# Forgetting attention's raw weights in ten large buffers, and the weights' bound by GpSimd's queue

## The chip, the cores and the metric

The kernel runs on one core of a Trainium2 chip. Its time is that of the device, in microseconds (us): the median of several runs of the whole program. Five engines work side by side, each through its own queue in order: TensorE (PE, matrix products), VectorE (DVE), ScalarE (ACT), GpSimd (POOL) and SyncE (SP, which here only issues transfers). An instruction waits at the head of its queue for the semaphores it names; what stands behind it waits too.

## The reference: what is computed

Two layers over a sequence of 1024 tokens with 1024 channels, batch 1. Each layer projects `x` into a main part, queries for the memory and gates, computes a main branch and a memory branch, multiplies both by the gates, projects back and normalises:

```python
h = x @ w_in                      # [u_main | q_mem | g_main | g_mem], 3072 columns
y_main = main_fn(u_main)
y_mem = memory_attention(q_mem, mem, w_mem_kv)       # 4 heads, 256 memory tokens
y = concat([y_main * silu(g_main), y_mem * silu(g_mem)])
x = layer_norm(ALPHA * x + y @ w_out)
```

In layer 0 `main_fn` is a pooling over the last 2, 4, 8 and 16 tokens by groups of 256 channels, with a linear map for each group. Then `x @ w_kv_shared` gives keys, values and the logits of the forget gates for 16 heads of 64 channels. In layer 1 `main_fn` is forgetting attention: `logit[t, s] = q_t . k_s / 8 + cum[t] - cum[s]`, causal, where `cum` is the running sum of the logarithms of the forget gates.

## The kernel before

**Products in parts.** A float32 product is made as a sum of products of parts: a value is cut into a high part and a rest. In layer 0 that is `hi` with `lo` and `top` (`hi_lo`: a cast on ACT, a subtraction on DVE L187, a cast on ACT L188). In layer 1 both operands are scaled by powers of two and cut into two 16-bit halves (`Half`); the scale of the weights, `sw`, comes from a bound on all of that layer's weights.

**A slab** (L272) is 128 columns of a projection for all 1024 tokens: the weights come as two pieces of 128x512 float32, 256 KB each, and 48 products of 512 columns (L294) go to two banks of PE's accumulators (`pj`), 24 to each. `split_w` (L195) loads a piece by SP's queue into `raw`, a ring of four buffers of 2 KB a partition (L114), and cuts it into `w`, a ring of six (L117).

**The bound** (`look_ahead` L219, `bound_of` L231). The 84 pieces of weights behind the bound are loaded once more ahead of their use: each comes into `raw` by SP (L223), and ACT takes absolute values with their sum (L224, an instruction and a read of its accumulator). They are called for in portions: five behind each slab of memory queries (L412), three at each step of the memory attention, three behind a gate's slab, six behind a group, and what is left at the bound itself. `bound_of` then reduces them on DVE, writes a column to DRAM (L236), reads it back to all partitions (L238) and reduces again. `scales_of` (L244) calls it at the start of layer 0's output projection (L558), ahead of its products (L534).

**Layer 0** does pooling group 0, the memory attention, pooling groups 1 to 3 and the output projection; the weights of the projection are cut ahead of time in portions of 4, 12 and 12 (`out_proj.split`) into buffers that are free (`wtags`). **Layer 1** does the memory attention, then the forgetting attention (`fox`, 16 heads in 8 pairs). There a flag `low[0]` makes POOL cut the weights (`gp_scaled_hi_lo`): it scales a piece in place (L170), copies the high half (L181) and subtracts (L172). 27 slabs are cut so: keys, values and queries of the pairs, and their gates. POOL also makes the causal masks in `R` (L884), which the custom instruction on DVE that adds the decay to the logits waits for (L892); ACT takes the exponential (L900), ACT and DVE make two 16-bit halves (L921, L922), SP issues their transposes `T<-P` (L935), and PE multiplies by the values (L944).

**Order.** Forgetting attention and memory attention run under a schedule in which PE's order is written by hand: the products of the slabs are spread between the heads' steps (`Fill.pump`), and the gates of pairs 3, 5 and 6 (`late_gate`) fill the last pair's steps. The orders of the other engines come from a scheduler that works on the program as a whole. Ten buffers named `B` of 4 KB a partition serve layer 1: results of the memory attention's queries, and at the end the weights of the output projection.

Of the kernel before, what the change touches and what calls it, by code (L numbers as in the profile page):

```python
# [18 lines left out]
P = 128  # L19
# [54 lines left out]
def trunk_kernel(ctx, tc, x, xT, memT, win, wk, wv0, wv, wmk, wmv, wout, poolw, pscale, lng, lnb, bforget, out):  # L74
# [39 lines left out]
    def raw(shape):  # L114
        return sb(list(shape), "raw", 4)
# [7 lines left out]
    def w_slots(tags, where):  # L123

        def tiles(k):
            tag, bufs = tags[k]
            if tag == "w":
                return [parts_of(wt, [P, NH]) for _ in range(2)]
            two, four = [P, 2, NH], [P, 2, 2, NH]
            if tag == "MK":  # L130
# [61 lines left out]
        nc.gpsimd.tensor_tensor(to.lo, src, to.hi.bitcast(F32), ALU.subtract)  # L192
        gp_copy(to.top, src)

    def split_w(src_dram, shape, sc=None):  # L195
        r = raw(shape)
        nc.sync.dma_start(r, src_dram)
        if sc is not None:
            to = half_of(wt, shape)
            (gp_scaled_hi_lo if low[0] else scaled_hi_lo)(to, r, sc)  # L200
            return to
        to = parts_of(wt, shape)
        (gp_hi_lo if low[0] else hi_lo)(to, r)
        return to
# [11 lines left out]
    sums = const.tile([P, len(ahead)], F32, name="sums")  # L216
    seen_of = iter(enumerate(ahead))

    def look_ahead(n):  # L219

        for k, src in islice(seen_of, n):
            r = raw(list(src.shape))
            nc.sync.dma_start(r, src)  # L223
            nc.scalar.activation(r, r, AF.Abs, accum_out=sums[:, k : k + 1])  # L224

    def power_of(to, m, least):

# [2 lines left out]

    def bound_of(m):  # L231

        look_ahead(len(ahead))
# [10 lines left out]
    def scales_of(gb):  # L244

        other = tiny(1)
        nc.vector.tensor_reduce(tmp, gb[0], AX.X, ALU.max, apply_absolute_value=True)
        nc.vector.tensor_reduce(other, gb[1], AX.X, ALU.max, apply_absolute_value=True)
        nc.vector.tensor_tensor(tmp, tmp, other, ALU.add)
        nc.vector.tensor_scalar(tmp, tmp, 32.0, None, ALU.mult)  # L250
        power_of(ex, tmp, 2.0 ** -2)
        nc.vector.reciprocal(sx, ex)
        nc.vector.tensor_scalar(sx, sx, 2.0 ** 13, None, ALU.mult)
        m = tiny(1)
        bound_of(m)
# [16 lines left out]
    def slab(pieces_dram, X, evac, banks=("pj", 2)):  # L272

        arrived = isinstance(pieces_dram, list)
        sc = sw if isinstance(X, Half) else None
        ws = list(pieces_dram) if arrived else [split_w(pieces_dram[0], [P, 4, P], sc)]
        accs = {}
        high, low_top = (0,), (1, 2)
        if arrived:
            order = [(n, pc, part) for pc in range(2) for n, part in ((0, high), (1, high), (1, low_top), (0, low_top))]  # L280
        else:
            order = [(0, pc, part) for part in (high, low_top) for pc in range(2)]
            order += [(1, pc, part) for part in (low_top, high) for pc in range(2)]
        seen = {0: 0, 1: 0}
        for n, pc, part in order:
            if len(ws) <= pc:
                ws.append(split_w(pieces_dram[pc], [P, 4, P], sc))
            if n not in accs:
                accs[n] = ps([P, NH], *banks)
            for i in part:  # L290
                a, b = three(ws[pc], X)[i]
                for k in range(4):
                    seen[n] += 1
                    nc.tensor.matmul(  # L294
                        accs[n], a[:, k, :], b[:, pc * 4 + k, n * NH : (n + 1) * NH],
                        start=seen[n] == 1, stop=seen[n] == 3 * KT,
                    )
                    if seen[n] == 3 * KT:
                        evac(slice(n * NH, (n + 1) * NH), accs[n])
                    yield NH  # L300
# [99 lines left out]
    def mem_attention(l, X, kv, qtile, ytile, yd):  # L400
# [6 lines left out]
        for h in range(MH):  # L407
            while turns:
                spread()
            q = parts_of(qtile, [P, S])  # L410
            run(slab(win[l, 8 + h], X, lambda cols, acc: q_split(l, q[:, cols], acc)))
            look_ahead(5)  # L412
            qs.append(q)
            if not l:
                keys(h)
            vals(h)
# [45 lines left out]
        with tc.manual_schedule(engines={PE}):  # L462
            for t in range(ST + 2):
                todo = [MVALUES if k in (5, 9) else 0 for k in range(t, ST + 2)]
                part = max(0, (fill.left + sum(todo)) / len(todo) - todo[0])
                if t < ST:
                    probs(t)
                look_ahead(3)
                fill.pump(part * 0.4)
                for h in range(MH):  # L470
                    if todo[0]:
                        values((t - 5) // 4, h)
                    fill.pump(part * 0.15)
            fill.pump(float("inf"))
# [4 lines left out]
    class OutProj:  # L479
# [3 lines left out]

        def __init__(self, l, wtile, yd):
            self.l, self.wtile, self.yd, self.ws, self.accs = l, wtile, yd, [{}, {}], None
            self.raws, self.n = [], 0

        def fetch_two(self, land):

# [29 lines left out]
        def products(self, accs, c, ys, apart=False):  # L519

            high, low_top = (0,), (1, 2)
            if apart:
                order = [(a, nh, part) for a in range(2) for part in (high, low_top) for nh in range(2)]
            else:
                order = [
                    (a, nh, part) for part in ((low_top, high) if c == 0 else (high, low_top))
                    for a in range(2) for nh in range(2)
                ]
            for a, nh, part in order:
                for i in part:  # L530
                    for k in range(4):
                        kt = 4 * c + k
                        y, w = three(ys[:, k, a * P : (a + 1) * P], self.ws[nh][kt // 2][kt % 2])[i]
                        nc.tensor.matmul(  # L534
                            accs[a][nh], y, w, start=kt == 8 and i == 0, stop=kt == 7 and i == 2,
                        )
                        yield NH

        def early(self, y, ys):
# [10 lines left out]
        def rest(self, resid, X, dst):  # L550
# [13 lines left out]
            for sp, c in order + [(sp, c) for sp in range(2, ST // 2) for c in (2, 0, 1)]:  # L564
# [5 lines left out]
                for k, _ in enumerate(self.products(accs[sp], c, ys, X is None and sp == ST // 2 - 1 and c == 1)):  # L570
                    if c != 2 and k % 6 == 5:
                        spread()
                if c == 1:
                    norm(sp, accs.pop(sp), gb, resid, X, dst)

# [56 lines left out]
    y1d = dram.tile([3, P, 4, S], F32, name="y1d")  # L632

    with tc.tile_pool(name="in0", bufs=1) as in0:

        def bt(shape=(P, S), dt=F32R):
            return sb(list(shape), "B", 8, dt, in0)

        def pool_group(g):
# [25 lines left out]
            for f in (2 * g, 2 * g + 1):  # L665
                y = sb([P, S], "Y", 4, F32, in0)
                run(gate_units(win[0, 12 + f], y, X))
                if g:
                    look_ahead(3)
                ys.append(y)  # L670
            for d in range(2):
                f = 2 * g + d
# [19 lines left out]

        X1 = half_of(stream, [P, KT, S])
        out_proj.rest(x, X1, x1)
# [3 lines left out]
    with tc.tile_pool(name="in1", bufs=1) as in1:  # L698
# [432 lines left out]
```

## Time and profile before

| what | value |
|---|---|
| median of 3 runs | 1254.48 us (1251.09 to 1254.51) |
| the profiled execution | 1255.45 us |
| its span | 1253.7 us |
| granted clock of PE, mean over the span | 0.986 |
| PE / DVE / ACT / POOL busy | 95% / 65% / 58% / 17% |
| the 54 scales of POOL (L170) | 38.9 us busy, 123.6 us idle ahead of them |

The profile is one execution. Busy shares are means over stages with different limits: layer 0 takes the first 490 us or so (the last transposes of its result, L376, start at 492.8; the output projection begins at 344), forgetting attention lies between about 640 and 1130 us. In a row of a group stand the line, the engine, the operation, the result and its source, the shape, the count, the busy time, the mean duration in ns, and the idle time of the engine just ahead with what ended it. In a row of waits stand the waiting engine, its line and the releaser, then the total in us, the count and the longest. In a timeline's row stand the start, the duration, the engine, the operation and the count, and in brackets the idle time ahead of it. SPq is SP's queue, where a transfer is issued.

### The profile page before, as it was taken

What the parts mean: (1) busy time and instruction counts of PE and PEld (TensorE: products, weight loads), DVE (VectorE), ACT (ScalarE), POOL (GpSimd) and SP (SyncE); (2) the same over time, 40 slices, a digit from 0 to 9 for tenths busy, and PEclk for the clock granted to TensorE, in tenths of its full rate; (3) what the DMA queues carried; (4) which work ended last, traced back from release to release, by engine and by line L of the source; (5) the groups of instructions that cost most, each with busy time, mean ns of one, the idle gap of its engine ahead of it and who ended that gap; (6) DMA issues with size and microseconds to landing.
All of it is one profiled execution on the core that took longest, in us unless ns stands there. A gap on an engine that the chain in (4) does not pass through costs nothing. (4 is left out here: it accounts for less than half of the span.)

```text
span 1253.7 us, 20190 instructions
## 1 busy us (share of the span) xinstructions
PE 1185.7 (95%) x6970; PEld 685.0 (55%) x7018; DVE 811.0 (65%) x1882; ACT 730.3 (58%) x1596; POOL 218.9 (17%) x349
## 2 busy tenths in 40 slices
PE   8999998999999998999998989999998988999997
PEld 4566665555555556556664445544444454455553
DVE  7544656564735557357655887868877798773753
ACT  6577985675733235457323776767665776685220
POOL 4000000000000000000023443443443434440000
PEclk9999999999999999999999999998999999999999
DMA  6356885545573323345515787967886897886331
GB/s 227 108 181 190 211 211 176 182 138 186 163 202 101 105 108 129 96 134 103 166 55 144 155 161 176 184 144 160 158 173 136 177 181 172 200 225 203 134 139 46
DMA packets 279799, 195.61 MB, mean 156 GB/s; under 512 B 213776, under 2 KB 228368, under 8 KB 279696
## 3 DMA queue, kind: packets, MB, share of 16 engines
q1 hardware_dynamic: 279696, 194.31, 59.5%
q8 instruction: 55, 0.90, 0.3%
q14 instruction: 48, 0.39, 0.1%
HBM read 116.08 MB, written 22.61 MB: 111 GB/s over the span
## 5 line engine op out<-in xcount | busy, mean ns | idle before, releaser
L294 PE MATMUL pj<-A,w 128*128 128x512 f16 (+2 forms) x2908 | 674.1, 385 | 8.3 <-DVE A L822 2.9
L294 PEld LDWEIGHTS <-w 128*128 128x128 f16 (+1 forms) x2592 | 249.7, 98 | 291.8 <-issue 14.7
L900 ACT ACTIVATE T<-MK,s 128x512 f32<-128x512 f32 x192 | 111.0, 578 | 49.3 <-DVE P L922 27.2
L921 ACT ACTIVATE P<-T,s 128x512 f16<-128x512 f32 x192 | 102.6, 576 | 55.6 <-issue 19.5
L922 DVE SCALAR_TENSOR_TENSOR P<-T,s,P 128x512 f16<-128x512 f32 x192 | 111.4, 612 | 27.2 <-ACT P L921 25.0
L534 PEld LDWEIGHTS <-T 128*128 128x128 bf16 x736 | 71.0, 98 | 86.5 <-issue 6.3
L187 DVE TENSOR_TENSOR w<-raw,w 128x512 bf16<-128x512 f32 x84 | 59.8, 713 | 69.7 <-ACT w L186 48.8
L795 POOL MEMSET G<- 128x128 f32 x1 | 0.2, 205 | 597.8 <-PE T L270 597.8
L270 PE MATMUL L<-A 128*128 128x512 f16 (+3 forms) x384 | 86.0, 327 | 14.1 <-DVE s L892 13.9
L892 DVE CUSTOM_DVE_ANT_0 MK<-L,R,scales 128x512 f32<-128x512 f32 (+3 forms) x128 | 80.3, 627 | 9.5 <-PE L L270 5.9
L224 ACT ACTIVATE raw<-raw 128x512 f32<-128x512 f32 (+1 forms) x84 | 51.2, 610 | 57.5 <-DMA raw<-in_wv_dram 20.1
L294 PEld LDWEIGHTS pj<-A,w 128*128 128x128 f32 x368 | 69.0, 190 | 20.1 <-ACT A L186 3.1
L944 PE MATMUL O<-T,V 128*64 128x128 f16 (+1 forms) x1152 | 59.1, 224 | 15.3 <-DMA T<-P 13.1
L270 PEld LDWEIGHTS <-A 128*128 128x128 f16 x384 | 37.2, 98 | 58.6 <-issue 18.7
L944 PEld LDWEIGHTS <-V 128*64 128x64 f16 (+1 forms) x1152 | 52.2, 106 | 29.4 <-DMA T<-P 13.3
L186 ACT CAST T<-T 128x1024 fp32r<-128x1024 f32 x23 | 24.1, 1047 | 70.0 <-DMA T<-y1d 34.8
L172 POOL TENSOR_TENSOR w<-raw,w 128x512 f16<-128x512 f32 x54 | 63.3, 1173 | 3.7
L884 POOL TENSOR_SCALAR_AFFINE_SELECT R<-R 128x128 f32<-128x128 f32 x128 | 39.9, 317 | 131.1 <-DVE s L892 88.9
L187 DVE TENSOR_TENSOR T<-T,T 128x1024 bf16<-128x1024 f32 x23 | 28.0, 1218 | 50.9 <-ACT T L186 33.5
L186 ACT CAST w<-raw 128x512 fp32r<-128x512 f32 x84 | 51.9, 617 | 15.5 <-DMA raw<-in_win_dram 4.9
L170 POOL TENSOR_SCALAR raw<-raw,scales 128x512 f32<-128x512 f32 x54 | 38.9, 721 | 123.6 <-DMA raw<-in_win_dram 73.5
L892 DVE CUSTOM_DVE_ANT_0 MK<-L,R,s 128x512 f32<-128x512 f32 (+1 forms) x64 | 41.0, 641 | 25.3 <-POOL R L884 23.7
(263 smaller groups left out, 1852.2 us busy)
## 6 DMA issues: line engine op xcount, KB each, us to landing
raw<-in_win_dram SPq DMA_DIRECT2D x144, 256.0 KB, 3.0
raw<-in_wout_dram SPq DMA_DIRECT2D x40, 256.0 KB, 2.8
raw<-in_wk_dram SPq DMA_DIRECT2D x32, 256.0 KB, 2.9
R<-cumd SPq DMA_DIRECT2D x16, 512.0 KB, 4.6
y0d<-Y SPq DMA_DIRECT2D x12, 512.0 KB, 4.2
raw<-in_wv_dram SPq DMA_DIRECT2D x24, 256.0 KB, 3.2
T<-y0d SPq DMA_DIRECT2D x12, 512.0 KB, 3.8
T<-y1d SPq DMA_DIRECT2D x11, 512.0 KB, 4.7
```

The costliest lines, as they stand in the source:

```text
L172: nc.gpsimd.tensor_tensor(to.lo, src, to.hi, ALU.subtract)
L186: pin(nc.scalar.copy(to.hi, src))
L187: pin(nc.vector.tensor_tensor(to.lo, src, to.hi.bitcast(F32), ALU.subtract))
L224: nc.scalar.activation(r, r, AF.Abs, accum_out=sums[:, k : k + 1])
L270: nc.tensor.matmul(acc, a, b, start=i == 0, stop=i == len(terms) - 1)
L294: nc.tensor.matmul(accs[n], a[:, k, :], b[:, pc * 4 + k, n * NH : (n + 1) * NH], start=seen[n] == 1, stop=seen[n] == 3 * KT,)
L534: nc.tensor.matmul(accs[a][nh], y, w, start=kt == 8 and i == 0, stop=kt == 7 and i == 2,)
L892: nc.vector.tensor_tensor_reduce(p[:, lo:up], lg, R[:, lo:up], unq, top, ALU.add, ALU.min, m[:, n : n + 1])
L900: nc.scalar.activation(e, p[:, lo:up], AF.Exp, bias=top, scale=-1.0, accum_out=sums[:, n, hd % 2, i : i + 1],)
L921: nc.scalar.activation(pair[:, lo:up], e, AF.Copy, scale=r)
L922: nc.vector.scalar_tensor_tensor(pair[:, L + lo : L + up], e, r, pair[:, lo:up], ALU.mult, ALU.subtract)
L944: nc.tensor.matmul(acc[rows, (i % 4) * P : (i % 4) * P + P], v[:, b, 2 * j : 2 * j + (1 if e else 2), :].rearrange("p e d -> p (e d)"), pt ...
```

## The change

1. In forgetting attention a slab's two pieces land by one transfer of 512 KB on SP's queue in one of the ten large buffers `B` (`wide_raw`); `raw` isn't used for them any more. POOL cuts from there, with the same instructions. The products of a slab in layer 1 run in another order: all three parts of the first piece, then all of the second, for each half of the tokens.
2. The pieces for the weights' bound have two own buffers, `pre`, and are loaded by GpSimd's queue, two ahead. One piece is called for behind every 16th product of a slab in layer 0, and behind every 8th product of its output projection.
3. The weights' scales are taken out of `scales_of` into `scales_of_weights`, which is called late in layer 0's output projection, behind the products of row pair 2 with the second block, in place of ahead of the first.
4. In layer 0 the ring `W` has three buffers in place of four, one slot of the projection's weights lies in `W` and `P`, and 4, 10 and 10 pieces are cut ahead in place of 4, 12 and 12.

```diff
-    def split_w(src_dram, shape, sc=None):
-        r = raw(shape)
-        nc.sync.dma_start(r, src_dram)
+    roomy = []
+
+    def wide_raw():
+        return roomy[0]([P, 2, 4, P])
+
+    def split_w(src_dram, shape, sc=None, r=None):
+        if r is None:
+            r = raw(shape)
+            nc.sync.dma_start(r, src_dram)
...
-    def look_ahead(n):
-
-        for k, src in islice(seen_of, n):
-            r = raw(list(src.shape))
-            nc.sync.dma_start(r, src)
-            nc.scalar.activation(r, r, AF.Abs, accum_out=sums[:, k : k + 1])
+    landed, pre = [], [None]
+
+    def look_ahead(after=None, n=1):
+
+        for _ in range(n):
+            if landed:
+                k, r = landed.pop(0)
+                with tc.issue_after(after) if after else nullcontext():
+                    nc.scalar.activation(r, r, AF.Abs, accum_out=sums[:, k : k + 1])
+            while len(landed) < 2:
+                k, src = next(seen_of, (None, None))
+                if k is None:
+                    break
+                r = sb(list(src.shape), "pre", 2, F32, pre[0])
+                nc.gpsimd.dma_start(r, src)
+                landed.append((k, r))
...
+    def scales_of_weights():
+
         m = tiny(1)
         bound_of(m)
...
-        ws = list(pieces_dram) if arrived else [split_w(pieces_dram[0], [P, 4, P], sc)]
+        both = None
+        if low[0]:
+            both = wide_raw()
+            nc.sync.dma_start(both, pieces_dram.rearrange("c p k m -> p c k m"))
+        ws = list(pieces_dram) if arrived else [split_w(pieces_dram[0], [P, 4, P], sc, both and both[:, 0])]
...
-        if arrived:
+        if sc is not None:
+            order = [(n, pc, (0, 1, 2)) for n in range(2) for pc in range(2)]
+        elif arrived:
...
-                    nc.tensor.matmul(
+                    mm = nc.tensor.matmul(
...
+                    if sc is None and not arrived and sum(seen.values()) % 16 == 8:
+                        look_ahead(mm.ins)
...
-            look_ahead(5)
...
-                look_ahead(3)
...
+                        self.done += 1
+                        if not self.l and self.done % 8 == 0:
+                            look_ahead(mm.ins)
...
+                if X is not None and (sp, c) == (2, 1):
+                    scales_of_weights()
...
-        wtags = [("B", 8)] * 4 + [("W", 4)] * 2 + [("MK", 4), ("w", 0)] + [("Y", 4)] * 2 + [("PG", 0), ("MK", 4)]
+        wtags = [("B", 8)] * 4 + [("W", 3), ("WP", 0)] + [("MK", 4), ("w", 0)] + [("Y", 4)] * 2 + [("PG", 0), ("MK", 4)]
...
-            out_proj.split((4, 12, 12)[g - 1])
-            look_ahead(6)
+            out_proj.split((4, 10, 10)[g - 1])
...
+        roomy.append(land)
```

More of the change, by code (lines that the diff above doesn't have):

```diff
@@ L129, in tiles @@
             two, four = [P, 2, NH], [P, 2, 2, NH]
-            if tag == "MK":
+            if tag == "WP":
+                hi, pair = sb(two, "W", 3, F32R, where), sb(four, "P", 4, BF16)
+            elif tag == "MK":
                 hi, pair = MK(two), MK(four, BF16)
@@ L231, in bound_of @@
     def bound_of(m):
-        look_ahead(len(ahead))
+        look_ahead(None, len(ahead))
         line = dram.tile([P, 1], F32, name="line")
@@ L286, in slab @@
             if len(ws) <= pc:
-                ws.append(split_w(pieces_dram[pc], [P, 4, P], sc))
+                ws.append(split_w(pieces_dram[pc], [P, 4, P], sc, both and both[:, 1]))
             if n not in accs:
@@ L485, in __init__ @@
             self.l, self.wtile, self.yd, self.ws, self.accs = l, wtile, yd, [{}, {}], None
-            self.raws, self.n = [], 0
+            self.raws, self.n, self.done = [], 0, 0
         def fetch_two(self, land):
@@ L533, in products @@
                         y, w = three(ys[:, k, a * P : (a + 1) * P], self.ws[nh][kt // 2][kt % 2])[i]
-                        nc.tensor.matmul(
+                        mm = nc.tensor.matmul(
                             accs[a][nh], y, w, start=kt == 8 and i == 0, stop=kt == 7 and i == 2,
                         )
+                        self.done += 1
+                        if not self.l and self.done % 8 == 0:
+                            look_ahead(mm.ins)
                         yield NH
@@ L634, in trunk_kernel @@
     with tc.tile_pool(name="in0", bufs=1) as in0:
+        pre[0] = in0
         def bt(shape=(P, S), dt=F32R):
@@ L667, in pool_group @@
                 run(gate_units(win[0, 12 + f], y, X))
-                if g:
-                    look_ahead(3)
                 ys.append(y)
```

## The prediction

> **What bounds the kernel now.** I read the page's engine totals and the waits of TensorE (PE) first, then busy time by stage, then the waits of GpSimd (POOL) and the timelines around the longest stalls.
>
> ```profile
> PE 1185.7 (95%) x6970; PEld 685.0 (55%) x7018; DVE 811.0 (65%) x1882; ACT 730.3 (58%) x1596; POOL 218.9 (17%) x349
> ```
>
> ```profile
> PE L L270 <- DVE s L892: 13.9, 12, 2.9
> PE O L944 <- DMA T<-P: 13.1, 7, 3.0
> PE T L270 <- DMA T<-P: 5.0, 2, 4.1
> ...
> PE L L534 <- DVE T L187: 2.3, 1, 2.3
> ```
>
> ```profile
> 0.00:200.00 200.00, 187.42 (x1078) 121.25 (x1092) 111.71 (x233) 147.34 (x354) 14.45 (x15) 0.97 0.63 189
> ...
> 640.00:1130.00 490.00, 454.36 (x3086) 239.63 (x3086) 380.35 (x1054) 325.16 (x743) 199.29 (x326) 0.99 0.77 165
> ```
>
> PE is the bound: 95% busy, and no wait of its own is for a weight that POOL makes. What can be won is its idle time, 35.6 us of the 490 us of forgetting attention (490 less 454.36); what can be lost is whatever makes PE wait where it is full. In the last fence the columns after the length are PE, weight loads, VectorE (DVE), ScalarE (ACT) and POOL, then clock, DMA share and GB/s. ACT is busy 147.34 of the first 200 us, and only there is it close to a bound.
>
> **Part 1: ten large buffers in forgetting attention.** Two 256 KB loads into four small buffers become one of 512 KB into ten: 54 loads on SP's queue become 27. POOL's work stays (54 scales, copies and subtractions). What it costs today:
>
> ```profile
> POOL raw L170 <- DMA raw<-in_win_dram: 60.0, 21, 8.6
> POOL raw L170 <- DMA raw<-in_wv_dram: 26.6, 9, 7.8
> POOL raw L170 <- DMA raw<-in_wk_dram: 23.1, 8, 7.1
> ```
>
> ```profile
> 835.79 1.16 POOL L172 TENSOR_TENSOR w<-raw,w 128x512 f16<-128x512 f32 x1
> 844.87 0.69 POOL L170 TENSOR_SCALAR raw<-raw,scales 128x512 f32<-128x512 f32 x1 [7.92 <-DMA raw<-in_win_dram]
> 845.52 0.29 POOL L884 TENSOR_SCALAR_AFFINE_SELECT R<-R 128x128 f32<-128x128 f32 x1
> ```
>
> ```profile
> L892 DVE CUSTOM_DVE_ANT_0 MK<-L,R,s 128x512 f32<-128x512 f32 (+1 forms) x64 | 41.0, 641 | 25.3 <-POOL R L884 23.7
> ```
>
> ```profile
> 684.27 0.68 DVE L892 CUSTOM_DVE_ANT_0 MK<-L,R,s 128x384 f32<-128x384 f32 x1 [2.22 <-POOL R L884]
> ...
> 845.85 0.68 DVE L892 CUSTOM_DVE_ANT_0 MK<-L,R,s 128x384 f32<-128x384 f32 x1 [4.36 <-POOL R L884]
> ...
> 1040.62 0.54 DVE L892 CUSTOM_DVE_ANT_0 MK<-L,R,s 128x256 f32<-128x256 f32 x1 [2.06 <-POOL R L884]
> ```
>
> ```profile
> 846.59 0.80 PE L270 MATMUL L<-A 128*128 128x384 f16 x2 [2.93 <-DVE s L892]
> ```
>
> POOL waits 109.7 us in 38 places for a load, the causal mask stands behind it, DVE behind the mask, PE behind DVE. Of DVE's 23.7 us for masks, eight waits with 19.1 us have such a load ahead of the mask (the first, the longest and the last are shown). In the changed order the first ten slabs are loaded and scaled before the attention's first mask; of the next fourteen loads, placed by their neighbours' old times, all but two land before the mask behind them is due. So most of the 13.9 us goes, and some of the 13.1 us for transposes T<-P, which are late after such stalls. I take 9: 19.1 / 23.7 of the 13.9 is 11.2, less 2 for the two loads that stay. Ends: 0 (another wait steps in) and 27.0 (both rows). The new order of a slab's products (second piece wanted at the 13th product instead of the 5th, the first piece's low part at the 9th instead of the 13th) costs nothing while both pieces are scaled early; without that cover it is one subtraction, 1.16 us.
>
> The last three slabs are the other side. They are the gates of head pairs 3, 5 and 6, whose products fill PE during heads 14 and 15. Before, POOL scaled the first of them at 1038.86, ahead of need. In the changed order the large load of pair 3 stands on SP behind the transpose of head 14's third step, and the one of pair 6 behind that of head 15's fourth step. SP issues in order, so they leave when these do. Their old rows:
>
> ```profile
> 1074.72 1.70 SPq L935 DMA_TRANSPOSE T<-P  x1
> ...
> 1079.03 2.25 SPq L935 DMA_TRANSPOSE T<-P  x1
> ```
>
> ```profile
> 1105.28 1.00 DVE L922 SCALAR_TENSOR_TENSOR P<-T,s,P 128x384 f16<-128x384 f32 x2
> ```
>
> ```profile
> 1070.44 1.03 PE L294 MATMUL pj<-A,w 128*128 128x512 f16 x4
> ...
> 1084.75 0.59 PE L294 MATMUL pj<-A,w 128*128 128x512 f16 x2 [0.56 <-DVE G L307]
> ...
> 1099.82 1.03 PE L294 MATMUL pj<-A,w 128*128 128x512 f16 x4
> ```
>
> ```profile
> 1038.86 1.48 POOL L170 TENSOR_SCALAR raw<-raw,scales 128x512 f32<-128x512 f32 x2 [6.01 <-DMA raw<-in_win_dram]
> 1040.29 0.30 POOL L884 TENSOR_SCALAR_AFFINE_SELECT R<-R 128x128 f32<-128x128 f32 x1
> 1040.56 0.62 POOL L181 TENSOR_SCALAR w<-raw 128x512 f16<-128x512 f32 x1
> ```
>
> ```profile
> R<-cumd SPq DMA_DIRECT2D x16, 512.0 KB, 4.6
> ```
>
> The fourth product of the first and the last PE row is the first on the new weights: wanted at 1071.1 and 1100.5. Pair 3: load out at 1074.8, landed 4.6 later (the 512 KB row), both halves scaled (1.4: the row shows two in 1.48, the second's end hidden), copied (0.62): 1081.4, so PE stands 10.3 us. Pair 6: the transpose leaves when DVE has made its block, 1106.3; 1106.3 + 4.6 + 1.4 + 0.62 = 1112.9, so 12.4 us. Pair 5's load follows the transpose of 1079.03, 4 us after pair 3's, and its slab is wanted at 1084.75, 14 us after: nothing more. PE runs in the order written by hand and can do nothing else meanwhile, so both count in full: 22.7. Ends: 15 (DVE makes the blocks 3 us sooner after an undisturbed attention, loads land a microsecond sooner) and 29 (each load shares the engines for 3 us).
>
> At the end of the memory attention of layer 1 eight buffers come free together, and three large loads go out ahead of its last transpose, for which PE waits already:
>
> ```profile
> 613.02 0.49 PE L270 MATMUL T<-T,MK 128*128 128x128 f16 x6 [0.95 <-DMA T<-P]
> ```
>
> Between 0 and one such load's 4.6 us; I take 1.5.
>
> **Part 2: the bound's pieces by GpSimd's queue, in two own buffers.** 84 loads move from SP to POOL, whose queue holds little else here (14.45 us, x15). Each waits until ACT is done with the piece two before. On ACT the changed order doesn't hold the pieces back to every 16th product: they wait only for their load, and some 76 of the 84 stand before the old time 200.
>
> ```profile
> 0.00:200.00 200.00, 35.60 (x102) 0.97 0.63 189
> 200.00:330.00 130.00, 21.97 (x66) 1.00 0.48 160
> ```
>
> These are the pieces' own rows, two for each: 51 before 200 us now, 0.70 us apiece. With 76 ACT has 147.3 - 35.6 + 53.1 = 164.8 us of work in 200, so 35 us for waits. From the third piece on I summed the durations of ACT's rows between the end of the piece two before and the piece itself: 42 of 82 have under 3.0 us, 17 under 2.0. What a turn-round misses, added up in order: 24 us for a turn-round of 3.0, 36.5 for 3.5, 42.3 for 3.7, 52 for 4.0, 96 for 5.3. Behind a waiting piece ACT's queue holds evictions of PE's accumulators (two banks, 24 products each) and casts of weights, so ACT's lateness reaches PE after a few microseconds. ACT can't use all 35 us, since part is waiting for PE; I let it use 30. The turn-round has no row; the nearest are the same pieces by SP's queue:
>
> ```profile
> raw<-in_win_dram SPq DMA_DIRECT2D x144, 256.0 KB, 3.0
> ...
> raw<-in_memT_dram SPq DMA_DIRECT2D x8, 256.0 KB, 4.9
> ```
>
> I take 3.0 and 0.2 for two hand-overs and 0.5 for POOL to prepare the load, an estimate by its short instructions (0.29 to 0.69): 3.7, so 42.3 - 30 = 12 us. Ends: 0 (3.0) and 66 (5.3, the slow row with as much on top). The Trainium skill, DMA: Bandwidth & Descriptors, section Latency and other measured facts, gives the first byte at about 1 us on GpSimd's path and 0.6 on SyncE's; an estimate from that page is 3.6 for the turn-round and 9 us for the sum, and no run here shows it yet. Four pieces among the first casts of x are in the 12.
>
> **Part 3: scales, splits.** The bound's chain leaves the start of the output projection, where PE waits 2.3 us (L534 above). It returns near old time 425 with two transfers in a row and DVE behind them, ahead of layer 1: I take -1.5 (ends -2.3 and +3). Four weight pieces fewer split early and one W buffer less are put at nothing: DVE has room in that stage; without it, four subtractions of 0.73 us.
>
> ```profile
> L187 DVE TENSOR_TENSOR w<-raw,w 128x512 bf16<-128x512 f32 x44 | 32.1, 729 | 40.6 <-ACT w L186 26.5 <-PE pj L294 10.3 <-ACT raw L224 3.1
> ```
>
> **Sum.** The profiled execution took 1255.45 us (0.97 over the runs' median of 1254.48): 1255.45 - 9 + 22.7 + 1.5 + 12 - 1.5 = 1281.2; taken as 1281.
>
> **Rivals.**
> - *GpSimd's loads turn round like SP's.* The 12 falls away: 1269. For it: POOL is idle there. Against it: half the gaps are under 3.0 already.
> - *GpSimd's loads turn round in over 5 us.* 96 - 30 instead of 12: 1335; ACT becomes the bound of layer 0. A mechanism in this kernel would be DVE, busy 111.71 of those 200 us, holding up POOL's preparing of a load; against it, DVE's largest group there is a two-input operation (the row just above). The Trainium skill, SBUF — State Buffer, section Who interferes with whom, says that copies, casts and scalar forms of DVE can lock GpSimd out of the port by which it writes descriptors, and two-input ones not; no row here shows a load by GpSimd.
> - *Faster.* Masks free of loads and a shorter SP queue let DVE run ahead throughout, and PE's idle 35.6 us of attention go. That decides once it exceeds the other terms, 34.7 with GpSimd as I take it, 22.7 with GpSimd like SP: at its most 1255.45 - 35.6 + 22.7 + 1.5 - 1.5 = 1242.6. Against it: the waits with a cause here sum to 27.0.
> - *The change doesn't do what it says there:* no late load, since SP gets past the transposes early. Without the 22.7: 1258.5. Against it: PE has no other work before these products, and the transposes come from steps just before.
>
> **How the numbers follow.** Forecast 0.60, GpSimd like SP 0.20, over 5 us 0.10, faster 0.08, no late load 0.02. Cutting most of the third and of the faster case leaves 1260 to 1313, which takes in the ends of the late loads (-8, +6) and a turn-round up to 4.5. Within 0.3% (3.8 us, about what a measurement can tell) comes from the edge of the last two, 0.02. Faster 0.08, slower 0.90.
>
> **What would show it.** Right: PE waiting for POOL's L181-type copy twice, near the end of attention, 8 to 14 us each; POOL waiting for large loads there and hardly any mask behind one earlier; ACT's largest idle in layer 0 being for the pieces' loads, with PE idle beside it. Wrong: PE as full as before in 0 to 200 us (the 12), fewer than 15 us in the two late waits (the 22.7), or PE still waiting over 10 us for DVE's logits (the 9).

## The result, and the profile after

The changed kernel takes 1298.54 us (median; 1297.52 to 1303.03), the kernel before 1254.49 us beside it (1251.09 to 1257.89). The ratio is 1.0358, with an interval from 1.0321 to 1.0395: 3.6% slower. 1281 was forecast, with a range from 1260 to 1313. The profiled execution took 1299.03 us, its span is 1297.3.

The page of the changed kernel first: the engines' totals and the costliest group, the products of the slabs, with the idle time ahead of it at the end of its row.

```profile
PE 1201.4 (93%) x7018; PEld 691.4 (53%) x7018; DVE 815.1 (63%) x1882; ACT 730.9 (56%) x1596; POOL 265.2 (20%) x433
...
L321 PE MATMUL pj<-A,w 128*128 128x512 f16 (+2 forms) x2928 | 681.9, 387 | 33.2 <-POOL w L183 22.6
```

PE was 95% busy and is 93% busy. POOL has 84 instructions more (433 less 349) and 46.3 us more of busy time: the 84 loads, 0.55 us each. The last number is new: 22.6 us in which PE waited for POOL's copy of a weight, a releaser that did not appear among PE's waits before.

The waits of PE in the changed kernel (total, count, longest):

```profile
PE pj L321 <- POOL w L183: 22.6, 2, 11.5
PE O L976 <- DMA T<-P: 11.6, 6, 2.8
PE L L291 <- DVE s L924: 7.4, 9, 2.5
PE T L291 <- DMA T<-P: 5.8, 2, 3.6
...
PE pj L357 <- ACT w L190: 5.0, 5, 1.7
PE pj L321 <- ACT A L188: 5.0, 3, 2.6
PE pj L357 <- ACT B L190: 4.1, 4, 1.0
```

The wait for DVE's logits fell from 13.9 to 7.4, the way that was forecast. Waits for ACT's casts (L188, L190), twelve of at most 2.6 us, are now among the larger ones.

Where the 44 us arose is read from the two traces together. PE executes the same products in both; the table says how much later the product that began at a given time before begins in the changed kernel.

| begun before at | later by, us | stage that ends here |
|---|---|---|
| 290 | 28.6 | layer 0 without its output projection |
| 339 to 390 | 27.2 to 23.2 | start of the projection: the bound has gone from here |
| 594 | 22.9 | the rest of the projection, layer 1's queries and most of its memory attention |
| 662 | 29.5 | its last transpose and the first slabs of forgetting attention |
| 1058 | 18.6 | forgetting attention up to head 14 |
| 1106 | 43.5 | the late gates |
| the end | 43.6 | |

The busy time by stage, in the same order of columns as before: 0 to 200 us, attention, and the surroundings of the two late gates.

```profile
0.00:200.00 200.00, 175.41 (x937) 108.16 (x938) 96.79 (x202) 143.78 (x350) 49.08 (x83) 0.96 0.64 195
...
640.00:1130.00 490.00, 454.95 (x3117) 247.94 (x3116) 374.82 (x1031) 307.64 (x705) 181.60 (x299) 0.97 0.72 155
```

```profile
1090.00:1101.00 11.00, 0.00 (x0) 0.00 (x0) 6.48 (x16) 6.51 (x16) 3.13 (x6) 0.71 0.81 180
1101.00:1104.00 3.00, 2.65 (x22) 1.77 (x23) 0.00 (x0) 0.26 (x1) 3.00 (x4) 0.50 1.05 334
1104.00:1110.00 6.00, 6.00 (x29) 2.79 (x28) 3.51 (x8) 2.26 (x5) 5.99 (x9) 0.92 0.91 270
```

In the first 200 us PE is 12.0 us less busy than before (187.42 less 175.41), and ACT, which was to be fuller, is 3.6 us emptier although more of the pieces lie there: it waits. In the last fence PE stands for 11 us, and then 3 us go by at half the clock. The chain there, in the timeline of the changed kernel (start, duration, engine, line; in brackets the idle time ahead and what ended it):

```profile
1083.62 11.18 SPq L967 DMA_TRANSPOSE T<-P  x4
1094.85 0.90 SPq L300 DMA_DIRECT2D B<-in_win_dram  x1
...
1099.34 1.37 POOL L172 TENSOR_SCALAR B<-B,scales 128x512 f32<-128x512 f32 x2 [6.53 <-DMA B<-in_win_dram]
1100.68 1.21 POOL L183 TENSOR_SCALAR w<-B 128x512 f16<-128x512 f32 x2
1101.35 0.61 PE L321 MATMUL pj<-A,w 128*128 128x512 f16 x1 [11.46 <-POOL w L183]
...
1125.29 10.55 SPq L967 DMA_TRANSPOSE T<-P  x4
1135.89 0.64 SPq L300 DMA_DIRECT2D B<-in_win_dram  x1
1140.36 1.37 POOL L172 TENSOR_SCALAR B<-B,scales 128x512 f32<-128x512 f32 x2 [2.81 <-DMA B<-in_win_dram]
1142.37 0.61 PE L321 MATMUL pj<-A,w 128*128 128x512 f16 x1 [11.13 <-POOL w L183]
```

Four transposes take 11.18 us to be issued, from 1083.62; right behind them SP sends the load at 1094.85; it is there at 1099.34; POOL scales both halves and copies one; PE starts at 1101.35. The second time the load stands behind four transposes again (1125.29 and the 10.55 us in which they were issued).

The pieces in layer 0 (first row: ACT's instructions, shortest, median and longest, first and last start; below it ACT's idle time ahead of them by what ended it, and its count):

```profile
L235 ACT ACTIVATE pre<-pre x84: 425/629/642, 10.9 to 241.0; 128x512 f32<-128x512 f32 x76, 128x272 f32<-128x272 f32 x8
...
  DMA pre<-in_win_dram: 31.4, 25
  DMA pre<-in_wv_dram: 17.8, 11
...
  DMA pre<-in_wk_dram: 9.1, 7
```

ACT waited 58.3 us for pieces. Before, they stood between 48.5 and 324.1 us:

```profile
L224 ACT ACTIVATE raw<-raw x84: 426/629/647, 48.5 to 324.1; 128x512 f32<-128x512 f32 x76, 128x272 f32<-128x272 f32 x8
```

In attention, GpSimd's waits for weights and DVE's for masks (the changed kernel, 668 to 1155 us):

```profile
POOL B L172 <- DMA B<-in_win_dram: 27.4, 8, 6.5
POOL B L172 <- DMA B<-in_wk_dram: 21.7, 4, 13.1
POOL B L172 <- DMA B<-in_wv_dram: 19.7, 4, 7.4
```

```profile
DVE MK L924 <- POOL R L916: 11.8, 7, 4.1
```

POOL waits 68.8 us in 16 places (109.7 in 38 before), and DVE's waits for masks are 11.8 us in 7 places. And the end of layer 1's memory attention:

```profile
638.54 0.80 PE L291 MATMUL T<-T,MK 128*128 128x128 f16 x6 [3.56 <-DMA T<-P]
639.13 2.77 PE L291 MATMUL O<-T,MK 128*128 128x128 f16 x24
```

The wait for the last transpose was 0.95 us and is 3.56.

### The profile page after: what moved, and what is told of

Its sections match the earlier page's. It is cut to its first block, busy times and chain, and to the rows that moved or that the text cites. A ratio compares the mean times of both kernels' runs of the same rounds, so it can differ in the third digit from the quotient of the medians.

```text
span 1297.3 us, 20232 instructions
## 1 busy us (share of the span) xinstructions
PE 1201.4 (93%) x7018; PEld 691.4 (53%) x7018; DVE 815.1 (63%) x1882; ACT 730.9 (56%) x1596; POOL 265.2 (20%) x433
## 5 line engine op out<-in xcount | busy, mean ns | idle before, releaser
L321 PE MATMUL pj<-A,w 128*128 128x512 f16 (+2 forms) x2928 | 681.9, 387 | 33.2 <-POOL w L183 22.6
L932 ACT ACTIVATE T<-MK,s 128x512 f32<-128x512 f32 x192 | 111.0, 578 | 49.0 <-DVE s L924 28.6
L172 POOL TENSOR_SCALAR B<-B,scales 128x512 f32<-128x512 f32 x54 | 41.3, 777 | 464.0 <-ACT B L427 332.0
L924 DVE CUSTOM_DVE_ANT_0 MK<-L,R,scales 128x512 f32<-128x512 f32 (+3 forms) x128 | 80.3, 628 | 10.9 <-PE L L291 8.3
L235 ACT ACTIVATE pre<-pre 128x512 f32<-128x512 f32 (+1 forms) x84 | 51.3, 611 | 58.5 <-DMA pre<-in_win_dram 31.4
L976 PE MATMUL O<-T,V 128*64 128x128 f16 (+1 forms) x1152 | 62.2, 229 | 13.0 <-DMA T<-P 11.6
L976 PEld LDWEIGHTS <-V 128*64 128x64 f16 (+1 forms) x1152 | 54.9, 109 | 27.6 <-issue 12.2
L174 POOL TENSOR_TENSOR w<-B,w 128x512 f16<-128x512 f32 x54 | 62.4, 1158 | 3.2
L188 ACT CAST w<-raw 128x512 fp32r<-128x512 f32 x84 | 52.0, 619 | 14.5 <-PE pj L321 4.5
L357 PE MATMUL pj<-T,w 128*128 128x256 bf16 (+1 forms) x384 | 49.4, 283 | 11.6 <-ACT w L190 5.0
L188 ACT CAST T<-T 128x1024 fp32r<-128x1024 f32 x23 | 24.1, 1047 | 57.3 <-PE pj L561 23.5
L190 ACT CAST w<-raw 128x512 bf16<-128x512 f32 x84 | 51.8, 617 | 6.2 <-PE pj L321 6.2
```

The source lines that it names most:

```text
L174: nc.gpsimd.tensor_tensor(to.lo, src, to.hi, ALU.subtract)
L188: pin(nc.scalar.copy(to.hi, src))
L190: (top or nc.scalar.copy)(to.top, src)
L321: mm = nc.tensor.matmul(accs[n], a[:, k, :], b[:, pc * 4 + k, n * NH : (n + 1) * NH], start=seen[n] == 1, stop=seen[n] == 3 * KT,)
L924: nc.vector.tensor_tensor_reduce(p[:, lo:up], lg, R[:, lo:up], unq, top, ALU.add, ALU.min, m[:, n : n + 1])
L932: nc.scalar.activation(e, p[:, lo:up], AF.Exp, bias=top, scale=-1.0, accum_out=sums[:, n, hd % 2, i : i + 1],)
```

## The experiments

The kernel before took 1259 to 1260 us beside the experiments, so they are compared by their ratio to it; "later by" means the same as in the table above. That lateness is read against one trace of the kernel before, an execution of 1255.45 us, so by the end it can hold up to some 5 us that the ratio doesn't. It also varies by itself: at old time 339 the changed kernel and the two below that share its layer 0 (late gates by small buffers, all slabs by small buffers) show 27.2, 29.6 and 31.1 us. Line numbers differ from kernel to kernel.

### The late gates

*The three late gates' weights by small buffers*, all else as in the changed kernel:

```diff
-        if low[0]:
+        if low[0] and not few[0]:
             both = wide_raw()
...
+            few[0] = True
             yield from gate_units(win[1, 12 + pr], g, X)
+            few[0] = False
```

> The changed kernel with one thing undone: the slabs of the last three gates (pairs 3, 5, 6) load by two small loads into the four small buffers again. Theory (the large loads stand behind late transposes on SP's queue): both waits of PE for POOL's copy, 22.6 us in sum, go, and with them some 2 us in which PE's granted clock was low behind the standstills: 1298.5 - 25 = about 1274. Rival (the standstill is POOL's own, the block of two slabs ahead of the mask): POOL is as late with small loads, and less than 10 us come back, 1289 or more.

Measured: 1276.34 us, ratio 1.0133 (1.0106 to 1.0160), against 1.0358. PE's waits from 1060 to 1140 us in this kernel:

```profile
PE O L976 <- DMA T<-P: 1.0, 1, 1.0
PE L L291 <- DVE s L924: 0.9, 2, 0.6
PE pj L321 <- DVE G L336: 0.7, 1, 0.7
```

POOL's copy is not among them, and the lateness stays at 21.0 us through to the end instead of rising by 25. The two waits are the work of the large loads behind the transposes, and nothing stepped into their place.

### Layer 0: the pieces

*The pieces held to their place on ACT.* In the changed kernel a piece's instruction is tied to a product of PE, but the piece runs on ACT, and the tie doesn't hold it back there: the 84 pieces run in one crowd up to 241 us. Here they keep their place in the program's order:

```diff
-                with tc.issue_after(after) if after else nullcontext():
-                    nc.scalar.activation(r, r, AF.Abs, accum_out=sums[:, k : k + 1])
+                tc.keep_in_program_order(nc.scalar.activation(r, r, AF.Abs, accum_out=sums[:, k : k + 1]))
```

> The changed kernel, but each absolute-value instruction is kept in program order on ACT, so that the 84 pieces spread over layer 0's slabs instead of crowding into the first 240 us; queue and buffers as changed. Theory (crowding times a turn-round of 3.7 us): ACT's waits no longer reach PE; the shift of 28.6 us against the kernel before, as seen at the start of the output projection, falls under 8, and the run takes about 1276. Rival (GpSimd's queue itself slows ACT or the other loads): the shift stays over 20, 1290 or more.

Measured: 1297.08 us, ratio 1.0280 (1.0225 to 1.0335): a miss as a whole; at 339 us it is 14.4 later, above the theory's 8 and below the rival's 20. Its pieces lie between 29.6 and 405.3 us, and the stretch it was made for is healed: PE is 1.2 us later at 143 us, where the changed kernel is 21. Busy time by stage in this kernel:

```profile
0.00:150.00 150.00, 144.19 (x737) 89.94 (x748) 77.98 (x157) 100.04 (x213) 26.94 (x39) 0.98 0.57 165
150.00:215.00 65.00, 47.32 (x357) 34.76 (x360) 36.99 (x79) 35.41 (x102) 4.93 (x9) 0.89 0.65 142
```

PE is 96% busy in the first and 73% in the second. There, in the memory attention, the pieces now stand ahead of exponentials on ACT, and the transposes made from these are late:

```profile
204.42 0.80 PE L290 MATMUL T<-T,MK 128*128 128x128 f16 x6 [9.31 <-DMA T<-P]
```

Another 9 us are lost between 364 and 390 us of the old time, in the output projection. There PE waits twice for DVE's first step of the normalisation (L616), 3.48 and 3.36 us. Ahead of the first wait DVE stands 7.52 us for a cast by ACT (L188), and ACT has stood 4.37 us for a piece's load ahead of that cast; ahead of the second, ACT stands 3.28 us for a piece with the normalisation's square root (L621) behind it. So spreading the pieces cures the slabs, and a fixed place for each moves the loss to the stages where ACT has no room.

*The pieces by SP's queue*, still two ahead in their own buffers and in a crowd:

```diff
-                nc.gpsimd.dma_start(r, src)
+                nc.sync.dma_start(r, src)
```

> The changed kernel with the pieces loaded by SP's queue instead of GpSimd's; two own buffers and an order on ACT about as crowded as in the changed kernel. Theory (crowding times turn-round): the turn-round falls from 3.7 to about 3.1 us, and the shift of layer 0 from 28.6 to 12 to 18: about 1285. Rival 1 (the queue is the cause): the shift is gone, about 1270. Rival 2 (only the order and the two buffers count, whichever queue): 1295 or more, or slower yet where a piece's load waits for ACT at the head of SP's queue with weights behind it.

Measured: 1284.24 us, ratio 1.0197 (1.0163 to 1.0232). PE is 12.3 us later at 242 us and 11.0 at 339, where the changed kernel is 28.6 and 27.2. ACT's idle time ahead of pieces, and the first 200 us:

```profile
  DMA pre<-in_win_dram: 24.7, 23
  DMA pre<-in_wv_dram: 14.0, 11
...
  DMA pre<-in_wk_dram: 5.8, 4
```

```profile
0.00:200.00 200.00, 183.56 (x998) 115.12 (x1012) 105.46 (x225) 151.74 (x372) 14.10 (x15) 0.99 0.68 198
```

44.5 us of waits in place of 58.3, and PE some 8 us busier in the first 200. At 339 us that is 16 us less than in the changed kernel (19 to 20 less than in the two that share its layer 0 and were run beside this one), and 11 stay. The theory's 12 to 18 fits about, neither rival does.

### Attention: the buffers and the order of products

*Small buffers for all slabs of attention*, with the rest of the change:

```diff
-        if low[0]:
+        if False:
             both = wide_raw()
```

> The changed kernel without its large buffers: all 27 slabs of forgetting attention load by two small loads into the four small buffers again; the new order of a slab's products stays, and so does all of layer 0. Theory: the late waits (25 us) go, the three large loads ahead of the memory attention's last transpose go (6), and the 11 us that forgetting attention had won are lost: 1298.5 - 25 - 6 + 11 = about 1278. Rival (the 11 us come from the order of the products, not from the buffers): they stay, about 1268.

Measured: 1291.83 us, ratio 1.0259 (1.0231 to 1.0287): a miss by some 10 us by the ratio. The late waits and the loss at the last transpose are gone, as expected, but attention loses 11.7 us against the kernel before (26.0 later at 645 us, 37.7 at 1106). DVE's waits for masks and PE's for logits in this kernel:

```profile
DVE MK L924 <- POOL R L916: 36.0, 20, 4.6
```

```profile
PE L L291 <- DVE s L924: 18.3, 15, 3.5
```

Both are above those of the kernel before (26.3 and 13.9), with the same small buffers. What differs is the order of a slab's products.

*The new order alone, in the kernel before:*

```diff
-        if arrived:
+        if sc is not None:
+            order = [(n, pc, (0, 1, 2)) for n in range(2) for pc in range(2)]
+        elif arrived:
```

> The kernel before with the new order of a slab's products in layer 1 and nothing else. With all loads small again the attention was about 12 us longer than in the kernel before, though its loads were the same; what differed there was this order. If the order is the cause (the first piece's low half is wanted at the 9th product, not the 13th): 9 to 13 us slower than the kernel before, about 1.008 to 1.010 of it. Rival (other side effects of the change: four small buffers shared otherwise, later loads of the output projection's weights): within 3 us of the kernel before.

Measured: 1266.11 us, ratio 1.0059 (1.0039 to 1.0079), 7.4 us by the ratio, below the 9 to 13 that were expected and far over the rival's 3. The trace has it in attention (1.5 us later ahead of it, 10.2 behind it), so 8.7 of the 11.7 us, through the same waits:

```profile
DVE MK L894 <- POOL R L886: 35.9, 21, 4.7
```

```profile
PE L L270 <- DVE s L894: 17.0, 13, 3.1
```

Why DVE waits longer under this order is argued only: the order calls for the second piece at the 13th product instead of the 5th, so its load is asked for later, and POOL waits longer for it with the masks behind.

### A version faster than both

*Large buffers, late scales and the new order kept; the pieces again in the old portions, by SP into `raw`; the late gates by small buffers.* The portions are called for at their old places:

```diff
     def look_ahead(n):
         for k, src in islice(seen_of, n):
-            r = sb(list(src.shape), "pre", 2, F32, pre[0])
-            nc.gpsimd.dma_start(r, src)
+            r = raw(list(src.shape))
+            nc.sync.dma_start(r, src)
             nc.scalar.activation(r, r, AF.Abs, accum_out=sums[:, k : k + 1])
...
+            few[0] = True
             yield from gate_units(win[1, 12 + pr], g, X)
+            few[0] = False
```

> The changed kernel with the old look-ahead (pieces by SP into the four small buffers, in the old portions) and small loads for the last three gates; large buffers for the other 24 slabs, the weights' scales late. Theory (the parts add up: attention -11, the bound moved -5.4, loads ahead of the last transpose +6, layer 0's 28.6 and the late loads' 25 gone): 10 us faster than the kernel before, 0.992 of it. Rival (the gain in attention was only time that the late standstills gave back): no faster than before, 1.000 or more.

Measured: 1249.29 us, ratio 0.9920 (0.9894 to 0.9946). What is left in it of the changed kernel's losses is the last transpose:

```profile
612.30 0.80 PE L283 MATMUL T<-T,MK 128*128 128x128 f16 x6 [3.67 <-DMA T<-P]
```

PE is 3.4 us earlier than in the kernel before at 611 us, and 2.4 later at 645.

*In addition, the large loads wait until the last transpose has been issued:*

```diff
-            nc.sync.dma_start_transpose(
+            turned[:] = [nc.sync.dma_start_transpose(
...
-            nc.sync.dma_start(both, pieces_dram.rearrange("c p k m -> p c k m"))
+            with tc.issue_after(turned[0].ins):
+                nc.sync.dma_start(both, pieces_dram.rearrange("c p k m -> p c k m"))
```

> As the run before, and the first large loads are issued on SP behind the last transpose of layer 1's memory attention. Theory (three large loads ahead of that transpose make PE wait and run at a lower clock after): 5 to 6 us less than without it, about 0.987 to 0.988 of the kernel before. Rival (the transpose is late for another reason): no difference to the run before.

Measured: 1245.00 us, ratio 0.9892 (0.9855 to 0.9929). The same wait in this kernel:

```profile
606.46 0.49 PE L283 MATMUL T<-T,MK 128*128 128x128 f16 x6 [0.75 <-DMA T<-P]
```

From 611 to 645 us 2.5 us are lost in place of 5.8: three large loads ahead of the transpose on SP's queue are what made it late. The time is 4.3 us less by the medians; the intervals of the two ratios overlap. Run once more, beside the last two kernels of this section, it took 1245.17 us, ratio 0.9894 (0.9865 to 0.9923):

> The fastest version so far once more, as the reference for the two runs beside it: 0.987 to 0.992 of the kernel before.

*The same with the old order of products:*

> As the run before, with the old order of a slab's products. If the new order costs only where a piece is cut just ahead of use (small buffers): within 2 us of the run before. If it costs in any case: 8 us less or more.

Measured: 1248.87 us, ratio 0.9914 (0.9889 to 0.9939), 3.9 us more by the medians; the intervals of the two ratios overlap, but eight of its nine executions lie above all four of the run before. So with the large buffers the new order costs nothing that these runs show and may gain a little, and with the small ones it costs 7 us. The likely reason, argued and not shown: a slab's two pieces arrive together, and the place of the second in the order no longer asks for a load.

*The fastest kernel with the pieces by GpSimd's queue* (portions and `raw` kept):

```diff
             r = raw(list(src.shape))
-            nc.sync.dma_start(r, src)
+            nc.gpsimd.dma_start(r, src)
```

> The fastest version so far (old look-ahead, held loads, small loads for the last three gates) with the 84 pieces loaded by GpSimd's queue, into the four small buffers and in the old portions; ACT's order is the same but for a few neighbours. Theory (GpSimd's queue is slower by 0.4 to 0.7 us a load, which four buffers and sparse pieces hide): within 3 us of the version with SP. Rival (the queue itself, its loads or POOL's issue, is what layer 0 paid for): 10 us or more slower.

Measured: 1258.09 us, ratio 0.9990 (0.9970 to 1.0010): a miss, and what the rival said: 12.9 us slower by the medians than with SP's queue. In this kernel ACT's idle time ahead of pieces that wait for their load, and SP's wait, from 0 to 345 us, for a buffer of `raw` that a piece holds:

```profile
  ACT raw L234: 84.4, 42
```

```profile
SPq L205 <- ACT raw L234: 91.2, 25, 13.5
```

And the same rows of the fastest kernel, as it was run beside this one:

```profile
  ACT raw L234: 56.3, 40
```

```profile
SPq L205 <- ACT raw L234: 26.3, 21, 4.0
```

ACT waits 84.4 us in place of 56.3, and SP's own loads of weights, which share the four buffers, wait 91.2 us in place of 26.3. The four kernels make a table of the lateness at old time 339, the start of the output projection:

| | by GpSimd's queue | by SP's queue |
|---|---|---|
| one by one, in a crowd, two own buffers | 27.2 | 11.0 |
| in portions, spread, four shared buffers | 17.7 | 0.9 |

Each of the two changes costs by itself, the queue 16 to 17 us and the crowd some 10, and together they about add up. The 17.7 comes from an execution 5 us above its kernel's median, so its lateness may be nearer to 13, and the 27.2 is 29.6 and 31.1 in the two kernels with the same layer 0: the queue's share lies between 12 and 20, the crowd's between 10 and 18. How much of the crowd's 10 is the order and how much the number of buffers was not taken apart.

*The fastest kernel with the scales at their old place*, at the start of the output projection:

> The fastest version so far with the weights' scales at their old place, at the start of layer 0's output projection. Theory (the two transfers of the bound hold up DVE and SP just where the projection starts): 4 to 6 us slower than without, all of it by the projection's first 40 us. Rival (the bound's chain was hidden but for 2.3 us): 1.5 to 2.5 us slower.

Measured: 1248.12 us, ratio 0.9907 (0.9876 to 0.9939), 3 us more by the medians, with intervals that overlap: between the theory and the rival. In the trace it is 7.7 us behind the fastest kernel at old time 390 and 3.1 at the end. DVE stands 7.93 us for the bound's transfer back, and after that PE waits 3.68 us for DVE's normalisation, which it doesn't in the fastest kernel. So the trace has the late scales worth several microseconds where they stand; part of that is given back in attention, by a way that was not settled.

The fourth part of the change, fewer pieces cut ahead and a smaller ring `W`, has no run of its own. It is in the four kernels of this section that load the pieces by SP's queue in portions, and these are within 1.5 us of the kernel before at old time 339, so it costs little up to there.

## Why the prediction was right, and where it was not

The direction, the two late waits and the range were right; the time was 17.5 us short. The largest loss was not the late gates, as in the sum, but layer 0, whose term is 16.6 too small. The other terms miss by up to 5 us each, in both directions, and that these about cancel is luck.

- **Two late gates, 22.7: right.** PE waited 11.46 and 11.13 us, 22.6 together, where 10.3 and 12.4 stood. The chain was the one described: transpose, load, two scales, copy. Not in the sum was the clock afterwards: the lateness rises by 24.9, 2.3 more than the two waits. The rival "no late load" falls, and with the gates by small buffers the loss is gone.
- **Attention's masks, -9: right in size, with one thing missing.** From 662 to 1058 us 10.9 us were won. The waits named carry most of it: in that stretch DVE's for masks fell (26.3 to 11.8 us over the whole attention), and PE's for logits with them by 6.1, for transposes by 1.5. The sum had worked out its 9 from the logits alone. The sentence that the new order "costs nothing while both pieces are scaled early" holds with the large buffers; its price without that cover was put at one subtraction, 1.16 us, and is 7.4 us for the kernel. Against small buffers under the same order the large ones are worth some 23 us from 645 to 1058 us (13.4 lost with the small, 9.9 won with the large).
- **The last transpose, 1.5: mis-sized.** The wait is 3.56 us, and with what lies behind it, a clock of 0.59 from 640 to 645 us among it, 6.6 us are lost in all from 594 to 662. The upper end had been one load's 4.6. Held back behind the transpose, the loads leave a wait of 0.75.
- **The pieces in layer 0, 12: mis-sized; it was 28.6.** The turn-round itself was right: forecast 3.7 us, and over the 42 pieces from the third on for whose load ACT stood waiting, the median from the end of the piece two before to the start of the next is 3.67. (Over all 82, from that end to the landing it is 3.60, of which 0.40 until the load is issued.) The place of the pieces was right too: 75 of them start before the time that was 200. What failed is the step ahead of the turn-round, the work that covers it. It was summed from the durations of ACT's rows, and in the trace these overlap: a cast of 0.60 us is followed by the next after 0.51.

```profile
69.44 0.60 ACT L188 CAST T<-raw 128x512 fp32r<-128x512 f32 x1
69.95 0.61 ACT L190 CAST T<-raw 128x512 bf16<-128x512 f32 x1
70.47 0.61 ACT L188 CAST T<-raw 128x512 fp32r<-128x512 f32 x1
```

Summed as in the prediction, the changed kernel's own rows cover under 3.0 us in 38 of the 82 gaps, and a turn-round of 3.7 misses 40.5 us, close to the forecast's 42 gaps and 42.3 us. With overlapping time counted once it is 55 gaps and 56 us, and with each load's own turn-round 63; ACT waited 58.3. So the double count accounts for most of the missing 16 us, and the spread of the loads adds some 7 to that sum: on the page, 48 of them take 3.1 us from issue to landing, and 28, those of the keys' and values' weights, 4.0 and 4.1. The first pieces came late as well: the second load left at 15.03 us, behind POOL's copies of x.

The second half of the step, that ACT can spare 30, fits here (58.3 less 30 is 28.3) and about as well with the pieces by SP's queue (44.5 us of waits, 11 lost), but not where the pieces are spread: in the fastest kernel ACT waits 56.3 us and 0.9 are lost. The sum of the waits doesn't say what they cost; what it comes down to, as the waits of PE for casts by ACT (L188, L190) in the profile after suggest, is whether something that PE needs soon stands behind the waiting piece.
- **The bound, -1.5: mis-sized.** Between 339 and 390 us 4.0 us were won, and 5.4 from 290 on; near its new place, by 425, nothing is lost.
- **The rivals.** GpSimd turning round like SP's, which was to leave no loss in layer 0: the medians differ little (3.60 and 3.48 us to the landing), but even by SP's queue the crowd costs 11. Turn-rounds over 5 us throughout: no, and preparing a load kept POOL 0.55 us as a rule and 0.73 at most, so DVE held it up little. Faster: DVE does wait less for masks, and the losses exceed that gain by far; with them taken away the kernel is 1.1% faster than before.

The sum with what was measured in place of the terms: 28.6 - 5.4 + 6.6 - 10.9 + 25 = 43.9, and the end is 43.6 later.

## What to carry to other kernels

A larger buffer moves the time at which its load is asked for, and not always forward: go through every queue that the load is issued on and see what stands ahead of it at the last use, since a load behind a transpose that depends on the last step's result can't be early. Before side work is put on an engine's in-order queue, ask what stands behind each of its waits and not how long the waits are in sum. And judge the parts of a change one by one: here the large buffers of 24 slabs were worth keeping and the late scales probably, the queue, the crowd of pieces and the last three large loads weren't, and the sum hid both.

## What the runs showed of the hardware

A load by GpSimd's queue was issued 0.40 us (median) after the instruction that frees its buffer, one by SP's queue 0.03; from the issue to the landing the pieces took 3.19 and 3.23 us (the changed kernel, and the same with the pieces by SP's queue). The Trainium skill, DMA: Bandwidth & Descriptors, section Latency and other measured facts, gives GpSimd's path 0.4 us more to the first byte; here about as much shows, but ahead of the issue in the record and not in the landing. That the same loads by GpSimd's queue cost 12 us or more at equal medians was not expected. The medians hide a tail: in the fastest kernel the loads of the 84 pieces take 3.07 us on the mean from issue to landing and 4.8 at most by SP's queue, 3.86 and 10.6 by GpSimd's, 12 of them over 5 (in an execution 5 us above its kernel's median). What of the cost is the tail, what the hand-over and what the order of the queue stays open.

After PE had stood for 11 us its granted clock was 0.50 for 3 us and 0.92 over the next 6, in the changed kernel (the rows at 1101 and 1104 above): 0.92 over six is about one more at half, so the full clock is back some 3.6 us after PE's start at 1101.35. PE's stop of 3.56 us, from 634.98 to 638.54, has these rows around it:

```profile
635.00:640.00 5.00, 1.46 (x15) 1.46 (x15) 1.31 (x2) 0.16 (x1) 2.73 (x4) 0.73 1.13 220
640.00:645.00 5.00, 5.00 (x57) 5.00 (x56) 4.34 (x5) 0.00 (x0) 4.01 (x5) 0.59 1.03 397
```

By the same working the clock falls to half about 2.3 us after PE stops there, and is full again about 5.6 us after it starts; 24 products that took 1.50 us in the kernel before took 2.77 (the row at 639.13). The Trainium skill, TensorE: Matmul & The Clock Gate, section Part 1: The HAM clock gate, has half the clock after an idle window of about 3.4 us and the full one after as long a busy one. The return after the stop of 11 us agrees; at the shorter stop the fall came sooner and the return later. These three stops cost PE their length and some 1 to 3 us on top: 2.3 for the two long ones together, and 2.7 for the short one (from 611 to 622 us the lateness rises by 5.3, and the wait is 2.6 longer than before).
